# Batched float32 matmul: weight in 24 KB rows through three buffers, its casts cut into quarter-lane pieces on two engines

## The chip, the cores and the metric

One core of a Trainium2 chip runs the kernel. The metric is the device time of one execution in microseconds (us), the median over several runs. Engine names in the profile: PE is TensorE's matmuls, PEld its loads of the stationary operand, DVE is VectorE, ACT is ScalarE, POOL is GpSimd, SP is the queue that issues the transfers.

## The reference

```python
b1, b2, m, k, n = 8, 16, 256, 512, 384
x:      float32 [8, 16, 256, 512]
weight: float32 [8, 16, 512, 384]
np.matmul(x, weight).astype(np.float32)      # 128 independent 256x512 by 512x384 products
```

The inputs are 167.8 MB and the output 50.3 MB.

## The kernel before

It works on groups of G = 4 matrices, 32 groups in all. Each group goes through these steps: SP loads weight (two transfers of 1.5 MB, 12 KB per partition) and x (2 MB, 16 KB per partition); ScalarE casts x to bf16; TensorE transposes it (bf16 pairs as float32 words); VectorE casts the weight and copies ("evacuates") the transposes to `x_t`; TensorE multiplies, four matrices side by side with 32 columns each; ScalarE copies the result out of the accumulators; SP stores it (1.5 MB, 12 KB per partition). The parts that the change touches:

```python
    XS, WS, OS = 2, 2 * G // D, 4        # buffers of x, half groups of weight (D = 2), out
    BS, TS, WBS = 1, 2, 2 * G
    LAG = 4

    def load(e, t, U, s):
        n = t * U + s
        for d in range(G // D):                       # weight, two transfers
            slot = (s * (G // D) + d) % WS
            e.wait_ge(w_cast, ...)                    # the buffer's last casts are done
            e.dma_start(w_sb[slot][:], w_rows[...].rearrange("(p k) n -> p k n", k=S * KO))...
        e.wait_ge(x_cast, n * T + (1 - XS) * T)
        e.dma_start(x_sb[s % XS][:], ...)             # x

    def prepare(e, t, U, s):                          # VectorE
        e.wait_ge(p_made, ...)
        for d in range(G // D):                       # all weight of group n: 8 casts of 64 lanes
            e.wait_ge(w_in[slot], ...)
            for a in range(D):
                for h in range(S):
                    e.tensor_copy(out=w_bf[...][h * HP : (h + 1) * HP], in_=w_sb[slot][...])
        for q in range(T):                            # then the transposes of group n
            e.wait_ge(t_made, n * T + (q + 1 + BIAS))
            e.tensor_copy(out=x_t[...], in_=pt[...])

    # ScalarE, per group: 4 casts of x n, then 4 copies of the products of n
    # TensorE, per group: 16 transposes, then 128 * 4 / 4 = 128 matmuls
    # SP, in a loop: load(n + LAG), then store(n)
```

## Time and profile before

| | before |
|---|---|
| time, median of 3 runs | 518.64 us (518.31 to 518.82) |
| span of the profiled execution | 517.2 us |
| share of the 16 DMA engines in use | 99.3% |
| VectorE, ScalarE, TensorE busy | 64%, 46%, 59% |

The row of the transfer queue says how much of the span packets were in flight, averaged over 16 DMA engines. A group row reads: line, engine, operation, out<-in, shapes, count | busy us, mean ns of one | idle time just before, and what ended it. The lines themselves are in the prediction below.

A transfer runs on 16 DMA engines, and its semaphore is complete only when the last of the 16 has landed. The trace records each of the 16 landings, but not which engine made it. No view of the profile prints these records; the figures for landings below are computed from the packed traces. I call the distance from the middle landing to the last one the **lag**, and the time from one last landing to the next, in queue order, the **late step** of a transfer. In the kernel before, the last x lands at 493.8 us on the middle engine and at 496.6 on the last one: a lag of 2.8 us.

### The profile page before, as it was taken

What the parts mean: (1) busy time and instruction counts of PE and PEld (TensorE: products, weight loads), DVE (VectorE), ACT (ScalarE), POOL (GpSimd) and SP (SyncE); (2) the same over time, 40 slices, a digit from 0 to 9 for tenths busy, and PEclk for the clock granted to TensorE, in tenths of its full rate; (3) what the DMA queues carried; (4) which work ended last, traced back from release to release, by engine and by line L of the source; (5) the groups of instructions that cost most, each with busy time, mean ns of one, the idle gap of its engine ahead of it and who ended that gap; (6) DMA issues with size and microseconds to landing.
All of it is one profiled execution on the core that took longest, in us unless ns stands there. A gap on an engine that the chain in (4) does not pass through costs nothing.

```text
span 517.2 us, 11523 instructions
## 1 busy us (share of the span) xinstructions
PE 306.6 (59%) x4608; PEld 200.6 (39%) x4608; DVE 332.8 (64%) x384; ACT 236.7 (46%) x264; POOL 0.7 (0%) x6
## 2 busy tenths in 40 slices
PE   0478776556665457645577554776446765467752
PEld 0345444334443334433344332444324443244431
DVE  3698875667556676556675566855658656676550
ACT  0465564443644436435355354454444544544441
POOL 0000000000000000000000000000000000000000
PEclk9998877878777887878777778877788877778777
DMA  8999999999999999999999999999999999999996
GB/s 340 430 423 424 424 432 426 429 428 430 432 427 427 427 428 432 429 427 430 426 431 431 426 429 430 427 432 427 427 429 429 427 433 425 430 428 430 429 428 251
DMA packets 18869, 218.18 MB, mean 422 GB/s; under 512 B 2096, under 2 KB 2096, under 8 KB 2608
## 3 DMA queue, kind: packets, MB, share of 16 engines
q1 hardware_dynamic: 18864, 218.11, 99.3%
q8 instruction: 3, 0.05, 0.0%
q14 instruction: 2, 0.02, 0.0%
HBM read 167.77 MB, written 50.33 MB: 422 GB/s over the span
## 4 chain that ended last, share of the span: by engine, by line
DMA 81%; ACT 10%; PE 4%; issue 3%; ACTq 0%; SPq 0%
DMA x_sb<-in_x_dram 81%; ACT x_bf L132 9%; PE po L180 2%; PE pt L166 1%; ACTq L130 0%; ACT out_sb L194 0%; SPq L111 0%; SPq L103 0%; ACT L132 0%; ACTq L193 0%; SPq L282 0%; SPq L55 0%
## 5 line engine op out<-in xcount | busy, mean ns | idle before, releaser
L147 DVE CAST w_bf<-w_sb 64x1536 bf16<-64x1536 f32 x256 | 244.4, 955 | 47.2 <-DMA w_sb<-in_weight_dram 38.5
L166 PE MATMUL pt<-identity,x_bf 128*128 128x128 f32 x512 | 123.7, 425 | 199.3 <-ACT x_bf L132 199.1
L180 PE MATMUL po<-w_bf,x_t 128*32 128x384 bf16 x4096 | 185.1, 342 | 1.0 <-issue 1.0
L166 PEld LDWEIGHTS pt<-identity,x_bf 128*128 128x128 f32 x512 | 91.8, 216 | 232.1 <-issue 218.3
L194 ACT COPY out_sb<-po 128x768 f32<-128x768 f32 x128 | 102.2, 798 | 147.2 <-PE po L180 147.2
L153 DVE COPY x_t<-pt 128x1024 bf16<-128x1024 bf16 x128 | 88.4, 691 | 122.3 <-PE pt L166 121.8
L132 ACT CAST x_bf<-x_sb 128x1024 bf16<-128x1024 f32 x128 | 124.4, 1042 | 80.9 <-DMA x_sb<-in_x_dram 80.8
L180 PEld LDWEIGHTS po<-w_bf,x_t 128*32 128x32 bf16 x4096 | 108.8, 101 | 73.8 <-issue 14.2
L132 ACT ACT_TABLE_LOAD x8 | 10.3, 1283 | 42.9 <-DMA x_sb<-in_x_dram 42.9
masks.py:199 POOL TENSOR_SCALAR_AFFINE_SELECT identity<-identity 128x128 f32<-128x128 f32 x1 | 0.3, 292 | 0.2 <-POOL identity L200 0.2
L200 POOL MEMSET identity<- 128x128 f32 x1 | 0.2, 204 | 0.5 <-SPq L55 0.5
L271 POOL MEMSET const-bfloat16-1.0<- 128x1 bf16 x1 | 0.1, 101 | 0.0
L271 POOL MEMSET const-uint8-127<- 128x1 uint8 x1 | 0.1, 101 | 0.0
L271 POOL MEMSET const-float32-0.0<- 128x1 f32 x1 | 0.1, 98 | 0.2 <-issue 0.2
L271 POOL MEMSET const-float32-1.0<- 128x1 f32 x1 | 0.1, 98 | 0.0
## 6 DMA issues: line engine op xcount, KB each, us to landing
w_sb<-in_weight_dram SPq DMA_DIRECT2D x64, 1536.0 KB, 27.5
x_sb<-in_x_dram SPq DMA_DIRECT2D x32, 2048.0 KB, 27.5
out_dram<-out_sb SPq DMA_DIRECT2D x31, 1536.0 KB, 30.7
out_dram<-out_sb SPq DMA_DIRECT2D x4, 384.0 KB, 5.9
```

The source lines that it names most:

```text
L132: e.copy(out=x_bf[s % BS][:, rows], in_=x_sb[s % XS][:, rows].rearrange("p r (q s c) -> p r s q c", s=S, c=KO),).then_inc(x_cast, 1)
L147: e.tensor_copy(out=w_bf[(s * G + d * D + a) % WBS][h * HP : (h + 1) * HP], in_=w_sb[slot][a * HP : (a + 1) * HP, h * KO : (h + 1) * KO, : ...
L153: e.tensor_copy(out=x_t[s % TS][:, 2 * q : 2 * q + 2], in_=pt[(s * T + q) % PT][:].bitcast(bf16),).then_inc(t_copied, 1)
L166: ins = e.transpose(pt[(s * T + q) % PT][:, rr, h, :], words[:, 2 * q + rr, h :: KO // 2], identity[:],)
L180: ins = e.matmul(po[(s * T + q) % PO][mine, rr, :N], x_t[s % TS][:, 2 * q + rr, ko // 2, mine, ko % 2], w_bf[(s * G + i) % WBS][:, ko, :], ...
L194: e.copy(out=out_sb[s % OS][:, 2 * q : 2 * q + 2, :], in_=po[(s * T + q) % PO][:, :, :N],).then_inc(o_copied, 1)
L200: e.memset(identity[:], 0.0).then_inc(id_done, 1)
L271: nc = _bacc.Bacc("TRN2", target_bir_lowering=False, num_devices=1)
```

## The change

Intent: larger weight rows and weight further ahead of x, paid for with more and smaller casts shared by two engines. The group's weight comes in one transfer of 3 MB with 24 KB per partition into one of three buffers. With this layout a matrix lies on 32 partitions, so a cast covers a quarter of the lanes: 16 per group, 12 on VectorE and 4 on ScalarE. VectorE does one matrix of group n+1, then evacuates group n, then does the other three; ScalarE casts its quarter of weight n+1, then copies out group n, then casts x n+1. `x_t` has one buffer, out three.

```diff
-    XS, WS, OS = 2, 2 * G // D, 4
-    BS, TS, WBS = 1, 2, 2 * G
+    XS, WS, OS = 2, 3, 3
-    LAG = 4
+    LAG = 3
+    U = 6
...
+    def load_w(e, t, U, s):
+        n = t * U + s
+        if not isinstance(n, int) or n >= WS:
+            e.wait_ge(v_cast, (n - WS + 1) * (G * V))
+            e.wait_ge(a_cast, (n - WS + 1) * G)
+        e.dma_start(
+            w_sb[s % WS][:],
+            w_rows[bass.ds(n * (G * K), G * K)].rearrange("(p k) n -> p k n", k=G * KO),
+        ).then_inc(w_in[s % WS], 16)
...
+    def cast_w(e, cast, t, U, s, i, parts, done):
+        for h in parts:
+            cast(
+                out=w_bf[(s * G + i) % (2 * G)][h * C : (h + 1) * C],
+                in_=w_sb[s % WS][i * C : (i + 1) * C, h * KO : (h + 1) * KO, :],
+            ).then_inc(done, 1)
...
     # VectorE
+            for s in range(1, U + 1):
+                cast_w_start(e, t, U, s)             # waits for weight s to land
+                casts(t, U, s, range(1))
+                evacuate(e, t, U, s - 1)
+                casts(t, U, s, range(1, G))
...
     # ScalarE
+        def step(t, U, s, first=False):
+            cast_w_start(e, t, U, s)
+            for i in range(G):
+                cast_w(e, e.copy, t, U, s, i, range(V, G), a_cast)
+            if not first:
+                for q in range(T):
+                    copy_out(e, t, U, s - 1, q)
+            for q in range(T):
+                cast_x(e, t, U, s, q)
```

The order of SP stays: load weight, load x, store. The last group's weight comes in two halves.

More of the change, by code (lines that the diff above doesn't have):

```diff
@@ L43 @@
     T = R // 2
+    NG = B // G
+    V = G - 1
     D = 2
-    S = 2
-    HP = P // D
-    NG = B // G
-    XS, WS, OS = 2, 2 * G // D, 4
-    BS, TS, WBS = 1, 2, 2 * G
+    XS, WS, OS = 2, 3, 3
     PT, PO = 4, 2
-    LAG = 4
+    LAG = 3
+    U = 6
     ctx.enter_context(tc.tile_critical(no_gpsimd_drain=True))
@@ L72 @@
     x_sb = sbuf("x_sb", [P, R, K], fp32, XS)
-    x_bf = sbuf("x_bf", [P, R, S, HP, KO], bf16, BS)
-    x_t = sbuf("x_t", [P, R, KO // 2, P, 2], bf16, TS)
-    w_sb = sbuf("w_sb", [P, S * KO, N], fp32, WS)
-    w_bf = sbuf("w_bf", [P, KO, N], bf16, WBS)
+    x_bf = sbuf("x_bf", [P, R, K], bf16, 1)[0]
+    x_t = sbuf("x_t", [P, R, KO // 2, P, 2], bf16, 1)[0]
+    w_sb = sbuf("w_sb", [P, G * KO, N], fp32, WS)
+    w_bf = sbuf("w_bf", [P, KO, N], bf16, 2 * G)
     out_sb = sbuf("out_sb", [P, R, N], fp32, OS)
@@ L80 @@
     po = psum("po", [P, 2, 512], fp32, PO)
-    id_done, x_cast, w_cast, t_made, t_copied, p_made, o_copied = (
+    id_done, x_cast, v_cast, a_cast, t_made, t_copied, p_made, o_copied = (
         sems(name, 1)[0]
         for name in (
-            "id_done", "x_cast", "w_cast", "t_made", "t_copied", "p_made", "o_copied"
+            "id_done", "x_cast", "v_cast", "a_cast",
+            "t_made", "t_copied", "p_made", "o_copied",
         )
@@ L91, with load_x @@
     x_in, w_in, o_out = sems("x_in", XS), sems("w_in", WS), sems("o_out", OS)
+    w_last = sems("w_last", D)
     BIAS = 8
-    def load(e, t, U, s):
+    def load_x(e, t, U, s):
         n = t * U + s
-        for d in range(G // D):
-            slot = (s * (G // D) + d) % WS
-            if not isinstance(n, int) or n >= 2:
-                e.wait_ge(w_cast, n * (G * S) + ((d + 1) * D * S - 2 * G * S))
-            e.dma_start(
-                w_sb[slot][:],
-                w_rows[bass.ds(n * (G * K) + d * (D * K), D * K)].rearrange(
-                    "(p k) n -> p k n", k=S * KO
-                ),
-            ).then_inc(w_in[slot], 16)
         if not isinstance(n, int) or n >= XS:
-            e.wait_ge(x_cast, n * T + (1 - XS) * T)
+            e.wait_ge(x_cast, (n - XS + 1) * T)
         e.dma_start(
@@ L114, in load, with load_last @@
         ).then_inc(x_in[s % XS], 16)
+    def load_w(e, t, U, s):
[7 more added lines that the diff above has]
+        ).then_inc(w_in[s % WS], 16)
+    def load(e, t, U, s):
+        load_w(e, t, U, s)
+        load_x(e, t, U, s)
+    def load_last(e):
+        n = NG - 1
+        e.wait_ge(v_cast, (n - WS + 1) * (G * V))
+        e.wait_ge(a_cast, (n - WS + 1) * G)
+        for d in range(D):
+            e.dma_start(
+                w_sb[n % WS][:, d * D * KO : (d + 1) * D * KO],
+                w_rows[bass.ds(n * (G * K) + d * D * K, D * K)].rearrange(
+                    "(p k) n -> p k n", k=D * KO
+                ),
+            ).then_inc(w_last[d], 16)
+        load_x(e, 0, NG, n)
     def store(e, t, U, s, pieces=1):
@@ L124, in store, with cast_x @@
             )
-    def cast_x(e, t, U, s, q):
+    def cast_x(e, t, U, s, q, S=G):
         n = t * U + s
@@ L132, in cast_x, with cast_w_start, cast_w_last, evacuate @@
         e.copy(
-            out=x_bf[s % BS][:, rows],
-            in_=x_sb[s % XS][:, rows].rearrange("p r (q s c) -> p r s q c", s=S, c=KO),
+            out=x_bf[:, rows].rearrange("p r (s q c) -> p r s q c", s=S, c=KO),
+            in_=x_sb[s % XS][:, rows].rearrange(
+                "p r (q s c) -> p r s q c", s=S, c=KO
+            ),
         ).then_inc(x_cast, 1)
-    def prepare(e, t, U, s):
+    def cast_w(e, cast, t, U, s, i, parts, done):
[4 more added lines that the diff above has]
+            ).then_inc(done, 1)
+    def cast_w_start(e, t, U, s):
         n = t * U + s
         e.wait_ge(p_made, n * T + (BIAS - T))
-        for d in range(G // D):
-            slot = (s * (G // D) + d) % WS
-            e.wait_ge(
-                w_in[slot], (t * (U * G // D // WS) + s * G // D // WS) * 16 + 16
-            )
-            for a in range(D):
-                for h in range(S):
-                    e.tensor_copy(
-                        out=w_bf[(s * G + d * D + a) % WBS][h * HP : (h + 1) * HP],
-                        in_=w_sb[slot][a * HP : (a + 1) * HP, h * KO : (h + 1) * KO, :],
-                    ).then_inc(w_cast, 1)
+        e.wait_ge(w_in[s % WS], (t * (U // WS) + s // WS) * 16 + 16)
+    def cast_w_last(e, cast, parts, done, by):
+        n = NG - 1
+        e.wait_ge(p_made, n * T + (BIAS - T))
+        H = P // D
+        for d, a in parts:
+            e.wait_ge(w_last[d], 16)
+            for h in range(D):
+                ins = cast(
+                    out=w_bf[(n * G + d * D + a) % (2 * G)][h * H : (h + 1) * H],
+                    in_=w_sb[n % WS][
+                        a * H : (a + 1) * H, (d * D + h) * KO : (d * D + h + 1) * KO, :
+                    ],
+                )
+        ins.then_inc(done, by)
+    def evacuate(e, t, U, s):
+        n = t * U + s
         for q in range(T):
@@ L153, in prepare, with transpose @@
             e.tensor_copy(
-                out=x_t[s % TS][:, 2 * q : 2 * q + 2],
+                out=x_t[:, 2 * q : 2 * q + 2],
                 in_=pt[(s * T + q) % PT][:].bitcast(bf16),
             ).then_inc(t_copied, 1)
-    def multiply(e, t, U, s):
+    def transpose(e, t, U, s, q):
         n = t * U + s
-        words = x_bf[s % BS][:].rearrange("p r s q c -> p r (s q c)").bitcast(fp32)
-        for q in range(T):
-            e.wait_ge(x_cast, n * T + (q + 1))
-            e.wait_ge(t_copied, n * T + (q + 1 - PT + BIAS))
-            for rr in range(2):
-                for h in range(KO // 2):
-                    ins = e.transpose(
-                        pt[(s * T + q) % PT][:, rr, h, :],
-                        words[:, 2 * q + rr, h :: KO // 2],
-                        identity[:],
-                    )
-            ins.then_inc(t_made, 1)
-        e.wait_ge(w_cast, n * (G * S) + G * S)
-        for q in range(T):
-            e.wait_ge(t_copied, n * T + (q + 1 + BIAS))
-            e.wait_ge(o_copied, n * T + (q + 1 - PO + BIAS))
-            for rr in range(2):
-                for ko in range(KO):
-                    for i in range(G):
-                        mine = slice(i * C, (i + 1) * C)
-                        ins = e.matmul(
-                            po[(s * T + q) % PO][mine, rr, :N],
-                            x_t[s % TS][:, 2 * q + rr, ko // 2, mine, ko % 2],
-                            w_bf[(s * G + i) % WBS][:, ko, :],
-                            start=(ko == 0),
-                            stop=(ko == KO - 1),
-                        )
-            ins.then_inc(p_made, 1)
@@ new lines, in transpose, with multiply @@
+        words = x_bf[:].bitcast(fp32)
+        e.wait_ge(x_cast, n * T + (q + 1))
+        e.wait_ge(t_copied, n * T + (q + 1 - PT + BIAS))
+        for rr in range(2):
+            for h in range(KO // 2):
+                ins = e.transpose(
+                    pt[(s * T + q) % PT][:, rr, h, :],
+                    words[:, 2 * q + rr, h :: KO // 2],
+                    identity[:],
+                )
+        ins.then_inc(t_made, 1)
+    def multiply(e, t, U, s, q):
+        n = t * U + s
+        if q == 0:
+            e.wait_ge(v_cast, n * (G * V) + G * V)
+            e.wait_ge(a_cast, n * G + G)
+        e.wait_ge(t_copied, n * T + (q + 1 + BIAS))
+        e.wait_ge(o_copied, n * T + (q + 1 - PO + BIAS))
+        for rr in range(2):
+            for ko in range(KO):
+                for i in range(G):
+                    mine = slice(i * C, (i + 1) * C)
+                    ins = e.matmul(
+                        po[(s * T + q) % PO][mine, rr, :N],
+                        x_t[:, 2 * q + rr, ko // 2, mine, ko % 2],
+                        w_bf[(s * G + i) % (2 * G)][:, ko, :],
+                        start=(ko == 0),
+                        stop=(ko == KO - 1),
+                    )
+        ins.then_inc(p_made, 1)
@@ L205, in on_sync @@
     def on_sync(e):
-        U = OS
         for n in range(LAG):
             load(e, 0, NG, n)
-        rounds = (NG - LAG) // U
+        rounds = (NG - 1 - LAG) // U
         with e.Fori(0, rounds) as t:
@@ L214, in on_sync, with casts @@
         for n in range(rounds * U, NG):
-            if n + LAG < NG:
+            if n + LAG < NG - 1:
                 load(e, 0, NG, n + LAG)
+            elif n + LAG == NG - 1:
+                load_last(e)
             store(e, 0, NG, n, T if n == NG - 1 else 1)
         for s in range(OS):
-            e.wait_ge(o_out[s], 16 + 16 * (NG // OS + (T - 1 if s == (NG - 1) % OS else 0)))
+            used = len(range(s, NG, OS)) + (T - 1 if s == (NG - 1) % OS else 0)
+            e.wait_ge(o_out[s], 16 + 16 * used)
     def on_vector(e):
-        U = 2
         e.sem_inc(t_copied, BIAS)
-        with e.Fori(0, NG // U) as t:
-            for s in range(U):
-                prepare(e, t, U, s)
+        def casts(t, U, s, matrices):
+            for i in matrices:
+                cast_w(e, e.tensor_copy, t, U, s, i, range(V), v_cast)
+        cast_w_start(e, 0, NG, 0)
+        casts(0, NG, 0, range(G))
+        with e.Fori(0, (NG - 2) // U) as t:
+            for s in range(1, U + 1):
[3 more added lines that the diff above has]
+                casts(t, U, s, range(1, G))
+        evacuate(e, 0, NG, NG - 2)
+        cast_w_last(e, e.tensor_copy, ((0, 0), (1, 0), (1, 1)), v_cast, G * V)
+        evacuate(e, 0, NG, NG - 1)
     def on_tensor(e):
@@ L236, in on_tensor @@
             for s in range(U):
-                multiply(e, t, U, s)
+                for q in range(T):
+                    transpose(e, t, U, s, q)
+                for q in range(T):
+                    multiply(e, t, U, s, q)
     def on_scalar(e):
-        U = OS
         e.sem_inc(o_copied, BIAS)
@@ L243, in on_scalar @@
             e.sem_inc(o_out[s], 16)
-        with e.Fori(0, NG // U) as t:
-            for s in range(U):
-                for q in range(T):
-                    cast_x(e, t, U, s, q)
-                for q in range(T):
-                    copy_out(e, t, U, s, q)
+        def step(t, U, s, first=False):
+            cast_w_start(e, t, U, s)
+            for i in range(G):
+                cast_w(e, e.copy, t, U, s, i, range(V, G), a_cast)
+            if not first:
+                for q in range(T):
+                    copy_out(e, t, U, s - 1, q)
+            for q in range(T):
+                cast_x(e, t, U, s, q)
+        step(0, NG, 0, first=True)
+        with e.Fori(0, (NG - 2) // U) as t:
+            for s in range(1, U + 1):
+                step(t, U, s)
+        cast_w_last(e, e.copy, ((0, 1),), a_cast, G)
+        for q in range(T):
+            copy_out(e, 0, NG, NG - 2, q)
+        for q in range(T):
+            cast_x(e, 0, NG, NG - 1, q, D)
+        for q in range(T):
+            copy_out(e, 0, NG, NG - 1, q)
     on_gpsimd(nc.gpsimd)
```

## The prediction

> **What bounds the kernel now.** I read the page from the top, then the chain, then stretches of the span, and last the packets. The page's share rows show that no engine is near its limit: TensorE is busy for 59% of the span, VectorE for 64%, ScalarE for 46%. The queue row is different:
>
> ```profile
> q1 hardware_dynamic: 18864, 218.11, 99.3%
> HBM read 167.77 MB, written 50.33 MB: 422 GB/s over the span
> DMA 81%; ACT 10%; PE 4%; issue 3%; ACTq 0%; SPq 0%
> ```
>
> The reader is to see 99.3%: packets were in flight for practically the whole span on all 16 DMA engines. The chain that ended last agrees, 81% of it is loads of x. Is there room at the ends? The view by stretches has the start, the middle, the time from the last landing of x, and the drain; the columns are the stretch, its length, the busy time of PE, PEld, DVE, ACT and POOL, the clock, the DMA share and GB/s:
>
> ```profile
> 0.00:20.00 20.00, 0.15 (x1) 0.16 (x2) 7.64 (x8) 2.62 (x3) 0.70 (x6) 1.00 0.89 369
> 60.00:260.00 200.00, 120.84 (x1853) 79.00 (x1846) 132.67 (x153) 94.60 (x106) 0.00 (x0) 0.79 1.01 429
> 260.00:460.00 200.00, 124.93 (x1844) 81.60 (x1848) 131.35 (x152) 92.98 (x104) 0.00 (x0) 0.78 1.01 429
> 496.50:507.70 11.20, 9.04 (x144) 6.26 (x144) 2.77 (x4) 7.06 (x8) 0.00 (x0) 0.79 1.00 425
> 507.70:513.50 5.80, 0.00 (x0) 0.00 (x0) 0.00 (x0) 0.02 (x1) 0.00 (x0) 0.82 0.75 305
> 513.50:517.20 3.70, 0.00 (x0) 0.00 (x0) 0.00 (x0) 0.00 (x0) 0.00 (x0) 0.50 0.03 13
> ```
>
> The middle runs at 429 GB/s with the DMA engines full, and even the last group's work (496.5 to 507.7) has full DMA beside it, as stores are still queued. Only some 2 us at the start, part of 5.8 us in the drain and a fixed 3.7 us at the end are not transfer. The bytes fix the rest: 218.1 MB at 429 GB/s is 508 us. One group of four matrices moves 3.146 MB of weight, 2.097 of x and 1.573 of out, so 7.33 + 4.89 + 3.67 = **15.9 us per group**. That is the period which every engine has to stay under, and 32 of them make the span.
>
> The waits of the transfer queue say the same from its other side: each load waits for a buffer, and then still takes 27.5 us to land where 1.5 MB need 3.7 us. It stands behind some 24 us of queued transfers; that is the slack which a late engine may use up before a DMA engine runs dry.
>
> ```profile
> SPq L103 <- DVE w_bf L147: 269.5, 60, 8.6
> w_sb<-in_weight_dram SPq DMA_DIRECT2D x64, 1536.0 KB, 27.5
> L147 DVE CAST w_bf<-w_sb 64x1536 bf16<-64x1536 f32 x256 | 244.4, 955 | 47.2 <-DMA w_sb<-in_weight_dram 38.5
> L153 DVE COPY x_t<-pt 128x1024 bf16<-128x1024 bf16 x128 | 88.4, 691 | 122.3 <-PE pt L166 121.8
> L132 ACT CAST x_bf<-x_sb 128x1024 bf16<-128x1024 f32 x128 | 124.4, 1042 | 80.9 <-DMA x_sb<-in_x_dram 80.8
> L194 ACT COPY out_sb<-po 128x768 f32<-128x768 f32 x128 | 102.2, 798 | 147.2 <-PE po L180 147.2
> ```
>
> **What the Trainium skill says.** (1) "DMA: Bandwidth & Descriptors", § Where 436 GB/s comes from, puts the fabric ceiling of 16 ports at 435 GB/s; the trace's 429 is 98.6% of it. (2) The same page, § Why small descriptors are slow (HBM only), gives about 3 cycles of overhead per packet, a loss for descriptors of a few hundred bytes. The trace agrees that there is nothing left at 12 KB: the packet records show a median of 460 ns for 12,288 B and 613 ns for 16,384 B, 0.0374 ns per byte in both. (3) "VectorE: DVE Perf Modes", § Two Vector instructions with no wait between them, says that an instruction whose start quadrant differs from the last one's is held until the earlier has finished. Quarter-lane casts change the output quadrant every time; but the half-lane casts of before do too, and eight of them take 7.86 us, 982 ns each against 955 ns alone. So I count 982 ns for a quarter-lane cast as well. (4) "ScalarE: Activation LUTs", § What ACT_TABLE_LOAD costs, gives 186 ns + 0.833 ns per element for a simple activation, and about 93 ns overlap back to back. For 1,024 elements that is 1,039 ns; the trace has 1,042.
>
> **The change, part by part.**
> *Transfers.* Weight comes as 32 loads of 3 MB in 24 KB rows (the last in two halves of 12 KB rows) in place of 64 of 1.5 MB in 12 KB rows. Bytes stay. By (2) a 24 KB packet should take 2 x 460 = 920 ns: gain about zero. Some 31 fewer transfers mean 31 x 16 = 496 fewer semaphore packets at 9 ns (packet records), over 16 engines 0.3 us. The order in the queue is still weight n, x n, store; one store fewer (LAG 3, was 4) now comes ahead of the last x.
> *VectorE.* A cast's length goes by its elements per lane, 1,536 in both, so halving the lanes doubles the count: 16 quarter casts per group, of which VectorE takes 12. Before, 8 x 0.982 + 4 x 0.69 = 10.6 us per group. After, 12 x 0.982 + 4 x 0.72 (0.69 and a small gap) = 11.8 + 2.9 = **14.7 us**, under 15.9.
> *ScalarE.* It gains 4 quarter casts. Estimate from the fit in (4): 186 + 0.833 x 1,536 = 1,466 ns, four of them 4 x 1.466 - 3 x 0.093 = 5.6 us. With 3.9 us for the four x casts (as the timeline shows them) and 4 x 0.8 = 3.2 for the copies, 12.7 us busy per group, before 7.1. Its order is now weight casts n+1, copies n, x casts n+1, so there is a loop through TensorE: weight casts 5.6; copies of two output tiles, the third and fourth tile only then made (1.35 us each), their copies: about 4.9; x casts 3.9. Together some **14.4 us** per group, plus 1.28 us of table load once in 6 groups. Under 15.9 again.
> *Where these lie.* Let x n land at time L. Weight n+1 lands one store and one weight load later, at L + 11. VectorE casts the first matrix until L + 14, evacuates the transposes until L + 17, casts the rest until L + 25.8; the next weight lands at L + 26.9. ScalarE casts until L + 16.7, copies until L + 21.5, casts x n+1 until L + 25.4, also in time. So both still wait for weight, with about 1.1 to 1.5 us to spare, and x is released 9.5 us after it landed in place of 4. The queue held some 24 us of work; that delay is absorbed. At the start five loads (13.6 MB, 32 us) are queued at once, and the third x is released at about 22 us by my count, before they run out.
> *The end.* One store fewer ahead of the last x: it lands 3.7 us later (about 500.2), with three stores queued behind it (11.0 us), in place of four. The last group's work took 11.2 us before (496.5 to 507.7) and its order is unchanged: last copy at about 511.4, its store's 0.9 us and a receipt of a few us after it. The transfers alone give 500.2 + 11.0 + 3.7 = 514.9, by the same sum as before (496.5 + 14.7 + 3.7). So the end moves by between 0 and +1 us.
>
> **Sum:** 518.6 - 0.3 (semaphore packets) + 0.3 (end, about a third of its width) + 0 (middle, bound by transfers) = **518.6 us**.
>
> **Rivals.**
> 1. *Larger rows lift the transfer rate.* The weight is 100.7 of 218.1 MB. For: it is what one would hope of 24 KB rows. Against: equal ns per byte at 12 and 16 KB, and only 6 GB/s left up to the ceiling in (1). Even at 435 GB/s for all bytes the gain is 508 - 501 = 7 us, 1.4%, still within 2%.
> 2. *VectorE or ScalarE becomes the bound.* For: 14.7 and 14.4 of 15.9 us leave some 8%, and the two engines now wait for each other through TensorE. A quarter cast of 1.1 us in place of 0.98 would make VectorE's group 16.1 us and the time some 525; ordering losses of 1.5 us a group, 32 x 0.5 = 16 us over the 1.0 to spare, give 530 to 535. If quarter casts lost their rate [...], VectorE would need over 20 us a group and the kernel some 700 us. Against: shape and layout in a lane are those of before, only lanes differ.
> 3. *Fewer buffers starve the queue* (out_sb 3 for 4, x_t 1 for 2). For: a store takes 30.6 us to land and out_sb is reused sooner. Against: by the schedule above a store is issued 25.4 us after its L and lands at about L + 51; the copy that reuses its buffer comes at L + 47.7 + 16.7, 13 us later. It would show as copies waiting for a store, and cost some us a group if it happened.
>
> **Range and chances.** The middle can hardly get faster: -2.6 us allows for slightly faster rows and a better drain. Above, +4 us allows a rougher start, a longer end or an occasional late engine. So 516.0 to 522.5 should hold it 8 times in 10. Faster by 2% needs under 508, below the bytes at today's rate with no start or end: 0.02. Slower by 2% (over 529) needs rival 2 or 3: 0.08. Within 2%: 0.90.
>
> **What would show it.** Right: DMA share of 1.01 and 428 to 431 GB/s in the middle; 24 KB packets at about 920 ns; VectorE at about (12 x 955 + 4 x 691) x 32 ns = 455 us busy, 88% of the span; ScalarE at 390 to 420 us; quarter casts still waiting for weight. Wrong: a DMA share clearly under 1.0 in the middle, VectorE over 95% busy, quarter casts on VectorE over 1.05 us or on ScalarE over 1.6 us, copies to out_sb waiting for stores, or transfer queue waits with landings well under 20 us.

## The result, and the profile after

The changed kernel takes **523.80 us** (median of 4 runs, 523.34 to 523.86), the kernel before 518.67 us in the same rounds. The ratio of the changed kernel to the kernel before is 1.0100 (95% interval 1.0085 to 1.0115). Ratios here are the mean time of one kernel's runs over that of the other's of the same rounds, so they are not quite the ratio of the medians. "Within 2%" was right; the time lies 1.3 us above the predicted range of 516.0 to 522.5, and 5.2 us above the predicted 518.6.

The page of the changed kernel, queue row, chain and groups:

```profile
q1 hardware_dynamic: 14400, 218.11, 98.0%
DMA 57%; PE 15%; DVE 9%; ACT 9%; issue 8%; SPq 1%; ACTq 0%; DVEq 0%
...
L163 DVE CAST w_bf<-w_sb 32x1536 bf16<-32x1536 f32 x372 | 353.8, 951 | 67.7 <-DMA w_sb<-in_weight_dram 56.9
...
L163 ACT CAST w_bf<-w_sb 32x1536 bf16<-32x1536 f32 x124 | 182.1, 1468 | 13.4 <-DMA w_sb<-in_weight_dram 10.5
```

A quarter-lane cast takes what was predicted: 951 ns on VectorE, 1,468 on ScalarE (estimate 1,466). VectorE is busy for 84% of the span, ScalarE for 79%. But the DMA share fell from 99.3 to 98.0%. The view by stretches (columns as in the prediction) says where:

```profile
60.00:260.00 200.00, 136.91 (x1808) 82.92 (x1808) 176.29 (x203) 164.93 (x154) 0.00 (x0) 0.76 1.01 430
260.00:460.00 200.00, 138.13 (x1836) 82.28 (x1840) 173.29 (x202) 160.30 (x150) 0.00 (x0) 0.74 1.01 431
...
500.00:512.00 12.00, 9.95 (x146) 6.32 (x144) 8.46 (x10) 9.01 (x10) 0.00 (x0) 0.79 0.55 230
512.00:522.10 10.10, 5.44 (x130) 3.36 (x128) 0.73 (x2) 3.19 (x4) 0.00 (x0) 1.00 0.41 162
```

The middle is as full as before, even a little faster (430 to 431 GB/s, was 429). The loss shows in the last 22 us, where the DMA engines are half idle; in the kernel before they were full until 507.7 us of 517.2. The timeline of the end (start, length, engine, group, and in brackets the idle time before it and what ended it), first the changed kernel and then the kernel before:

```profile
482.68 2.91 DVE L163 CAST w_bf<-w_sb 32x1536 bf16<-32x1536 f32 x3 [1.77 <-DMA w_sb<-in_weight_dram]
...
486.37 7.83 PE L222 MATMUL po<-w_bf,x_t 128*32 128x384 bf16 x128 [2.96 <-DVE x_t L192]
...
495.08 3.89 ACT L154 CAST x_bf<-x_sb 128x1024 bf16<-128x1024 f32 x4
...
507.12 3.89 ACT L154 CAST x_bf<-x_sb 128x1024 bf16<-128x1024 f32 x4
...
517.50 0.80 ACT L236 COPY out_sb<-po 128x768 f32<-128x768 f32 x1 [0.50 <-PE po L222]
```

```profile
496.66 3.89 ACT L132 CAST x_bf<-x_sb 128x1024 bf16<-128x1024 f32 x4 [3.83 <-DMA x_sb<-in_x_dram]
...
506.92 0.80 ACT L194 COPY out_sb<-po 128x768 f32<-128x768 f32 x1 [0.50 <-PE po L180]
```

The last copy ends at 518.3 us, not at the predicted 511.4. The chain to it starts with the weight of group 30, which VectorE receives at 482.7 us; from there matmuls 29, casts of x 30, matmuls 30, casts of x 31 and matmuls 31 follow each other. The landing records show why that weight is so late:

| landing, us | middle engine | second to last | last engine |
|---|---|---|---|
| weight 30, after | 474.6 | 476.7 | **482.7** |
| last x, after | 495.4 | 497.4 | **503.7** |
| last x, before | 493.8 | 495.7 | 496.6 |

Fifteen of the DMA engines are at most about 2 us behind the middle one, in both kernels. One is 8.3 us late in the changed kernel. Everything waits for it. That it is the same engine all the time is read from the lag, which grows steadily while the other fifteen keep together. The lag grows by about 0.27 us per group from group 8 on, and all of it in stores: in groups 10 to 26 the late step of a store is 3.96 us, the second to last engine's 3.70. Loads of weight and x take the late engine as long as the others.

The 4.9 us between the two spans add up from these records: the last x is preceded by one store more (+3.7 us), comes 2.1 us sooner on the middle engine (24 KB packets take 912 ns, twice 12 KB would be 920), and its lag is 8.3 in place of 2.8 us (+5.5). So it lands 7.2 us later (496.55 to 503.71). From there to the end it is 18.4 us in place of 20.6 (-2.2). Without the added lag the sum would be some 5.5 us smaller, an estimate that takes the other terms as they are.

### The profile page after: what moved, and what is told of

Read it like the earlier page. It is cut to its first block, busy times and chain, and to the rows that moved or that the text cites. A ratio compares the mean times of both kernels' runs of the same rounds, so it can differ in the third digit from the quotient of the medians.

```text
span 522.1 us, 11674 instructions
## 1 busy us (share of the span) xinstructions
PE 343.3 (66%) x4608; PEld 208.6 (40%) x4608; DVE 439.5 (84%) x506; ACT 412.6 (79%) x383; POOL 0.7 (0%) x6
## 4 chain that ended last, share of the span: by engine, by line
DMA 57%; PE 15%; DVE 9%; ACT 9%; issue 8%; SPq 1%; ACTq 0%; DVEq 0%
DMA w_sb<-in_weight_dram 57%; PE po L222 13%; DVE w_bf L163 6%; ACT x_bf L154 6%; DVE x_t L192 2%; ACT w_bf L163 2%; PE pt L204 1%; ACT out_sb L236 1%; SPq L106 1%; SPq L144 0%; ACTq L152 0%; SPq L116 0%; DVEq L191 0%; ACTq L314 0%; ACTq L170 0%
## 5 line engine op out<-in xcount | busy, mean ns | idle before, releaser
L163 DVE CAST w_bf<-w_sb 32x1536 bf16<-32x1536 f32 x372 | 353.8, 951 | 67.7 <-DMA w_sb<-in_weight_dram 56.9
L222 PE MATMUL po<-w_bf,x_t 128*32 128x384 bf16 x4096 | 227.6, 394 | 80.2 <-DVE x_t L192 76.5
L222 PEld LDWEIGHTS po<-w_bf,x_t 128*32 128x32 bf16 x4096 | 125.0, 115 | 182.2 <-DVE x_t L192 88.3
L163 ACT CAST w_bf<-w_sb 32x1536 bf16<-32x1536 f32 x124 | 182.1, 1468 | 13.4 <-DMA w_sb<-in_weight_dram 10.5
L204 PE MATMUL pt<-identity,x_bf 128*128 128x128 f32 x512 | 115.8, 382 | 93.9 <-ACT x_bf L154 93.6
L204 PEld LDWEIGHTS pt<-identity,x_bf 128*128 128x128 f32 x512 | 83.6, 213 | 126.2 <-issue 125.4
L154 ACT CAST x_bf<-x_sb 128x1024 bf16<-128x1024 f32 x128 | 124.4, 1042 | 0.8
L192 DVE COPY x_t<-pt 128x1024 bf16<-128x1024 bf16 x128 | 80.1, 684 | 5.5 <-PE pt L204 4.3
L180 DVE CAST w_bf<-w_sb 64x1536 bf16<-64x1536 f32 x6 | 5.7, 955 | 0.1
L180 ACT CAST w_bf<-w_sb 64x1536 bf16<-64x1536 f32 x2 | 2.9, 1469 | 0.0
```

The lines of the kernel that those rows point to most:

```text
L154: e.copy(out=x_bf[:, rows].rearrange("p r (s q c) -> p r s q c", s=S, c=KO), in_=x_sb[s % XS][:, rows].rearrange("p r (q s c) -> p r s q c ...
L163: cast(out=w_bf[(s * G + i) % (2 * G)][h * C : (h + 1) * C], in_=w_sb[s % WS][i * C : (i + 1) * C, h * KO : (h + 1) * KO, :],).then_inc(do ...
L180: ins = cast(out=w_bf[(n * G + d * D + a) % (2 * G)][h * H : (h + 1) * H], in_=w_sb[n % WS][a * H : (a + 1) * H, (d * D + h) * KO : (d * D ...
L192: e.tensor_copy(out=x_t[:, 2 * q : 2 * q + 2], in_=pt[(s * T + q) % PT][:].bitcast(bf16),).then_inc(t_copied, 1)
L204: ins = e.transpose(pt[(s * T + q) % PT][:, rr, h, :], words[:, 2 * q + rr, h :: KO // 2], identity[:],)
L222: ins = e.matmul(po[(s * T + q) % PO][mine, rr, :N], x_t[:, 2 * q + rr, ko // 2, mine, ko % 2], w_bf[(s * G + i) % (2 * G)][:, ko, :], sta ...
```

## The experiments

Seventeen profiles exist in all: before, after, and fifteen experiments. The variants of the changed kernel start from a form in which three waits of the SP queue are written as `n * T + constant`; `control` is that form alone. The runs went to four chips; the late engine showed on each.

This table holds what the runs gave. "In it" counts the matmuls that start within the late engine's store; late step and count are means over groups 10 to 26; lag is that of the last x. Runs marked "one run" have no interval. Three runs with many short instructions follow in the text, as their instructions do not last over groups 10 to 26.

| run | time, us | ratio to before | late step of a store, us | matmuls in it | lag, us |
|---|---|---|---|---|---|
| before | 518.7 | | 3.73 | 10 | 2.8 |
| after | 523.8 | 1.0100 | 3.96 | 62 | 8.3 |
| control | 523.8 | 1.0102 | 3.96 | 62 | 9.0 |
| rows12 | 526.3 | 1.0144 | 3.96 | 61 | 9.0 |
| no_act_w (one run, wrong result) | 523.2 | | 3.94 | 59 | 7.9 |
| dma24 (one run, wrong result) | 523.4 | | 3.70 | 0 | 1.8 |
| dma_pe (one run, wrong result) | 534.9 | | 4.09 | 91 | 13.5 |
| dma_act (one run, wrong result) | 638.9 | | 3.70 | 0 | 2.2 |
| dma_dve (one run, wrong result) | 523.8 | | 3.70 | 0 | 2.2 |
| evac_first (one run) | 520.0 | | 3.78 | 30 | 5.0 |
| store_mid | 521.3 | 1.0046 | 3.76 | 6 | 3.9 |
| store_mid_evac | 526.5 | 1.0144 | 4.01 | 63 | 10.4 |
| before_mid | 530.3 | 1.0231 | 4.15 | 86 | 14.3 |
| store_mid_tail | 518.8 | 1.0013 | 3.76 | 6 | 4.1 |

### First round: rows, ScalarE, or the DMA engines alone

**control**: waits rewritten, same values.

```diff
-            e.wait_ge(x_cast, (n - XS + 1) * T)
+            e.wait_ge(x_cast, n * T + (1 - XS) * T)      # and the two waits of load_w alike
```

> The changed kernel, with three waits of the transfer queue written as n*T + constant in place of (n - 1)*T: the same values, so the same schedule. It is the base of all variants. All theories: 523.3 to 524.2 us; last landing of the last x some 8 us behind the middle one of its 16 DMA engines (503.7 against 495.4 us).

It gave 523.78 us and a lag of 9.0 us: a fair base.

**rows12**: the same buffers, but two transfers of 12 KB rows per group.

```diff
-        e.dma_start(w_sb[s % WS][:], w_rows[...].rearrange("(p k) n -> p k n", k=G * KO))...
+        rows = w_rows[...].rearrange("(p k) n -> p k n", k=G * KO)
+        for d in range(D):
+            half = slice(d * D * KO, (d + 1) * D * KO)
+            e.dma_start(w_sb[s % WS][:, half], rows[:, half]).then_inc(w_in[s % WS], 16)
```

> The changed kernel with each group's weight loaded in two transfers of 12 KB rows into the same buffer, all else kept. Theory A (one of the 16 DMA engines falls behind, and the 24 KB rows are why): the lag of the last landing of the last x falls from 8.3 to about 3 us, and the time to 518.5 to 519.5 us. Theory A2 (one DMA engine falls behind for another reason): lag stays 7 to 9 us, time 523.5 to 525.5 us, as 12 KB rows cost 0.05 us more per group. Theory B (the end of the kernel is long because the last groups' work now comes after weight casts, whatever the landings do): 523.5 to 525.5 us whatever the lag is.

The lag stays at 9.0 us, so theory A falls: the row size is not the cause. The time rises by 2.5 us over control, 0.8 us more than the top of what A2 allowed; the middle engine's last x came 1.9 us later (497.3 for 495.4). That is what the 24 KB rows are worth.

**no_act_w**: ScalarE casts no weight.

```diff
-            for i in range(G):
-                cast_w(e, e.copy, t, U, s, i, range(V, G), a_cast)
+            e.sem_inc(a_cast, G)
```

> Wrong result on purpose: ScalarE casts no weight (the quarter of each weight that it made stays zero), but still waits for the weight to land. Takes 5.9 us per group off ScalarE. Theory A2 (lag comes from the DMA engines themselves): lag stays about 8 us, the last x still lands at about 503.5 us, and the time is 518.5 to 520.5 us as only what follows that landing is left (15 us). If ScalarE's reads of the weight buffers slow one DMA engine: lag under 4 us, time 516 to 518.5 us. Theory B alone: lag does not matter, 517 to 519 us.

The lag is still 7.9 us, so ScalarE's reads are not the cause. The time hardly moved (523.17, one run), which no theory had: with 5.9 us per group off ScalarE the last x still landed at 503.6 us, as A2 said, but its casts began only at 506.5, because VectorE still took its first cast of weight 30 at 482.6 us and evacuated group 29 behind it. The chain of the end hangs on the last landing of weight 30, not on ScalarE.

**dma24**: the changed kernel's transfers alone, paced by landings, no other engine at work. The result is zeros.

```diff
-            e.wait_ge(x_cast, ...)                     # load_x
+            e.wait_ge(x_in[s % XS], ...)               # load_w and store alike; on_vector, on_tensor
                                                        # and on_scalar are not called
```

> Wrong result on purpose (zeros): only the transfers of the changed kernel in the same order, from the same buffers, each paced by landings, with no other engine at work. Theory A or A2 with the cause in the DMA engines: the last engine's lag grows to 6 to 9 us by the last x and its stores take some 0.2 us longer than the others'. If the other engines' work causes the lag: it stays at 1.5 to 3.5 us. Time 512 to 518 us either way.

The stretches of this run (columns: stretch, length, POOL busy, clock, DMA share, GB/s):

```profile
0.00:10.00 10.00, 8.05 (x7) 1.00 0.00 0
...
260.00:460.00 200.00, 0.00 (x0) 1.00 1.01 431
460.00:521.60 61.60, 0.00 (x0) 1.00 0.95 405
```

The first 10 us clear the output tiles, so the transfers need some 511 us of the 521.6. With them the time missed the expected 512 to 518 us. The rate is the changed kernel's, and the lag is 1.8 us (one run): it does not come from the DMA engines by themselves. Something that goes with the other engines' work makes it.

### Second round: which engine does it

In the kernel before, late stores 28 and 29 took 4.04 and 4.00 us while the last matmuls ran, and store 30, after them, 3.71. In the changed kernel the matmuls of a group run right when the late engine stores. So the suspect was the coincidence of store and matmul. Three runs add one engine's work to dma24, back to back and with nothing waiting for it.

```diff
+    def on_tensor(e):                                  # dma_pe
+        with nc.Fori(0, 44, ...) as t:
+            ... 256 matmuls like the kernel's, on constant tiles
```

> Wrong result on purpose: the transfers alone, as in the run before, with TensorE doing the kernel's matmuls back to back on constant tiles all the while (nothing waits for it). So far: in the changed kernel one of the 16 DMA engines takes 3.95 us for a store where the others take 3.68, in the stores that coincide with matmuls and output copies; in the transfers alone none does. Theory C1 (matmuls, which read the on-chip memory, slow stores, which read it too): store steps of 3.85 to 4.0 us for the last engine or for all, its lag over 4 us by the end. C2 (ScalarE's output copies do it) or C3 (VectorE's casts do it): 3.65 to 3.72 us, lag under 2.5 us.

```diff
+    def on_scalar(e):                                  # dma_act
+        with e.Fori(0, 150) as t:
+            for q in range(T): e.copy(out=scratch[:, 2 * q : 2 * q + 2, :], in_=po[q % PO][:, :, :N])
```

> Wrong result on purpose: the transfers alone, with ScalarE copying from the accumulators to a tile of its own, back to back. C2: store steps of 3.85 to 4.0 us and a lag over 4 us. C1 or C3: 3.65 to 3.72 us and a lag under 2.5 us.

```diff
+    def on_vector(e):                                  # dma_dve
+        with e.Fori(0, 40) as t:
+            ... 12 casts like the kernel's quarter casts, from a tile of its own
```

> Wrong result on purpose: the transfers alone, with VectorE doing the changed kernel's quarter casts back to back from a tile of its own. C3: store steps of 3.85 to 4.0 us and a lag over 4 us. C1 or C2: 3.65 to 3.72 us and a lag under 2.5 us.

The stretches of dma_pe (columns: PE, PEld, DVE, POOL busy, clock, DMA share, GB/s):

```profile
260.00:460.00 200.00, 200.00 (x4930) 130.63 (x4924) 0.00 (x0) 0.00 (x0) 1.00 1.01 430
460.00:520.00 60.00, 8.33 (x208) 5.19 (x196) 0.00 (x0) 0.00 (x0) 0.60 0.91 389
520.00:533.00 13.00, 0.00 (x0) 0.00 (x0) 0.00 (x0) 0.00 (x0) 0.50 0.32 136
```

TensorE alone is enough. In stores 10 to 24, the ones that lie beside matmuls, the late step is 4.15 us with 100 to 104 matmuls in each; in the two after the matmuls had ended it is 3.67, so that the table's mean is 4.09. The lag is 13.5 us, and the run ends 11.5 us later than dma24 with one engine's backlog (32% of the DMA engines in use, then idle). Stores on the second to last engine run beside the same matmuls and take 3.70 us. ScalarE's copies and VectorE's casts leave the late step at 3.70 and the lag at 2.2 us. (The dma_act run is 638.9 us long only because I gave it too many copies; its transfers end at 521 us.) C1 stands in so far as it is TensorE; C2 and C3 fall.

**evac_first** changes the order on VectorE, so that the matmuls of group n do not wait for weight n+1.

```diff
-                cast_w_start(e, t, U, s)
-                casts(t, U, s, range(1))
-                evacuate(e, t, U, s - 1)
-                casts(t, U, s, range(1, G))
+                e.wait_ge(p_made, (t * U + s) * T + (BIAS - T))
+                evacuate(e, t, U, s - 1)
+                cast_w_start(e, t, U, s)
+                casts(t, U, s, range(G))
```

> The changed kernel with one change of order on VectorE: the transposes of group n are evacuated before the first cast of group n+1, not after it, so that the matmuls of group n need not wait for the weight of group n+1 to land. Theory D (this wait ties the matmuls to the last landing, so that the late engine's stores fall on them in every group): matmuls start some 3 us earlier, fewer of the late engine's stores coincide with them, lag 3 to 7 us, and the time 519 to 522.5 us. If the order is of no consequence: 523 to 524.5 us and lag 8 us. If VectorE loses more than it can spare (its slack is some 1.5 us per group): over 525 us.

As expected: 30 matmuls in the late store in place of 62, a late step of 3.78 us, lag 5.0, time 520.0 us (one run; before took 518.15 in one run on that chip). The first engine to land now had 55 matmuls in its stores and still took 3.64 us: being beside matmuls does not slow every engine.

### Third round: move the store, and what about the matmul it is

**store_mid** moves one issue: the store goes between weight and x.

```diff
-                load(e, t, U, LAG + s)
-                store(e, t, U, s)
+                load_w(e, t, U, LAG + s)
+                store(e, t, U, s)
+                load_x(e, t, U, LAG + s)
...                                                    # the tail after the loop alike
```

> The changed kernel with one issue moved: the store of group n goes into the transfer queue between the weight and the x of group n + 3, not after both. Theory C1 (matmuls slow the stores of one DMA engine where they coincide): the matmuls of a group start 3.7 us after the last landing of the next weight, so a store that directly follows that weight is over before them; the late engine's store step falls from 3.94 to 3.7 us, its lag at the last x from 8.3 to under 3.5 us, and the time to 517.3 to 519 us. If the lag has another cause, or is of no consequence for the time: 522.5 to 525 us.

The matmuls in a late store fall from 62 to 6, the late step to 3.76 us, and the lag to 3.9 us; 3.7 and under 3.5 were expected, and what the rest comes from was not tested. The time falls by 2.5 us to 521.26, less than the 517.3 to 519 expected. I had not counted that the last x now stands behind one store more: its casts waited for it until 503.6 us.

**store_mid_evac** puts both edits together.

> As store_mid, and VectorE evacuates the transposes of group n before the first cast of group n + 1, as in evac_first. Theory C1: matmuls start earlier, partly beside the store again: lag 2 to 5 us, time 516 to 519.5 us. It is the candidate to beat both kernels if the end gets shorter by more than the lag costs.

This miss is telling. Both edits help alone, and together they are worse than the changed kernel: 526.54 us, lag 10.4. The late engine's store now fills the 4 us right after the last landing of the weight (it ended 8.8 us after it in the changed kernel), and the matmuls start some 1 us after that landing in place of 3.7. So they meet again, with 63 matmuls in a late store and a late step of 4.01 us. The step goes with the count of matmuls in the store, whichever edit made it.

**dma_pe_short** has the same number of matmuls as dma_pe, with 32 moving columns in place of 384, so they run through in 115 us (7 to 122 us).

```diff
-                                po[q % PO][mine, rr, :N], ..., w_bf[0][:, ko, :],
+                                po[q % PO][mine, rr, :32], ..., w_bf[0][:, ko, :32],
```

> Wrong result on purpose: as dma_pe, with the same number of matmuls, but 32 moving columns each in place of 384, so TensorE executes as many or more instructions per us and reads a small part of the data per us. If the late engine is slowed by the reading of moving data: store step of the last engine 3.68 to 3.75 us and lag under 3 us. If by TensorE's instructions themselves, or their fetching or stationary loads: a step of 4.0 us or more while they run and a lag over 6 us.

In the two stores that lay wholly beside them the late step was 7.03 and 7.11 us, with 721 and 740 matmuls, and 3.69 us after them; the lag ended at 14.7. The time was 535.8 us (one run). The same number of instructions cost about the same lag as in dma_pe, with a twelfth of the moving data. It is not the moving data. The excess over 3.70 us, divided by the matmuls in the store, is 4.2 ns each in the changed kernel, 4.4 in dma_pe and 4.6 here, for counts from 62 to 740 (2.7 to 5.2 over all runs with 30 or more in a store).

### Fourth round: the other kernel, and instructions or memory

**before_mid** makes the store_mid edit in the kernel before.

> The kernel before, with its store moved between the weight and the x of the same loop step. Theory C1 (one DMA engine's stores are slowed by matmuls that run during them): before, the late engine's stores held 10 matmuls each (its step 3.73 us); moved to just ahead of the next x they fall on the previous group's matmuls, 5 to 10.5 us after the last x landed: over 40 matmuls in a store, a step of 3.85 to 3.95 us, and a lag at the last x of 5 to 9 us in place of 2.8. Time 519.5 to 523 us. If C1 is wrong: lag 2 to 3.5 us, time 518 to 519.5 us.

The kernel before becomes 12 us slower by moving one issue: 530.29 us, ratio 1.0231 (1.0214 to 1.0248). Lag and time went the way of C1 and far past my sizes. The matmuls follow the last landing, so the later the late engine is, the more surely they fall on its store: 86 on average. In the stretches of this run (columns as in the prediction) the end is drained by one engine:

```profile
500.00:512.00 12.00, 6.50 (x130) 3.54 (x128) 8.49 (x10) 3.57 (x5) 0.00 (x0) 0.78 0.68 285
512.00:528.50 16.50, 10.41 (x144) 6.52 (x144) 2.77 (x4) 6.76 (x8) 0.00 (x0) 0.71 0.28 111
```

**dma_pe_rows32** has the instructions of dma_pe_short on 32 partitions in place of 128.

```diff
-                                x_t[:, ...], w_bf[0][:, ko, :32],
+                                x_t[:32, ...], w_bf[0][:32, ko, :32],
```

> Wrong result on purpose: as dma_pe_short (its late engine fell back by some 12 us while 11264 short matmuls ran), with operands on 32 partitions in place of 128: the same number of TensorE instructions, a quarter of the on-chip memory read, none of it in three of four partition groups. Theory E (it is the instructions, for instance their fetching over the same DMA engine, and not what they read): lag 11 to 16 us as before. Theory F (what the stationary and moving loads read from on-chip memory slows a DMA engine that reads there): lag under 7 us.

The lag is 14.8 us again (late step 7.09 and 7.00 us in the two stores wholly beside them, 536.2 us in one run). Three quarters of the on-chip memory reads are gone and nothing changed, so theory F falls.

**dma_dve_short** lets VectorE run 5,120 copies of 8 elements.

```diff
+        with e.Fori(0, 40) as t:
+            e.wait_ge(a_cast, t * 128 + 128)
+            for i in range(128):
+                e.tensor_copy(out=scratch[1][:, i], in_=scratch[0][:, i]).then_inc(a_cast, 1)
```

> Wrong result on purpose: the transfers alone, beside 5120 tiny VectorE copies of 8 elements, some 70 to 100 ns each, on tiles of their own. Theory E in its wide form (any engine's instruction stream costs one DMA engine time during its stores, by its rate): one DMA engine falls back, by an estimate from dma_pe (0.41 us per store at some 50 instructions per us) of about 0.1 us per store at 12 per us: last store step 3.75 to 3.85 us while they run, lag 3.5 to 6 us. If only TensorE does this: step 3.70 us and lag under 2.5 us.

The row of these copies, 5,120 of them, busy for 381.5 us:

```profile
L167 DVE COPY scratch<-scratch 128x8 f32<-128x8 f32 x5120 | 381.5, 194 | 1.7 <-DVEq L163 0.3
```

The lag is 5.1 us, and the late step averages 3.85 us between 200 and 410 us. In dma_dve 480 large casts over more time left it at 3.70. So the number of instructions, of VectorE too, is what these runs point to: theory E in its wide form, for VectorE on one run of each kind.

**store_mid_tail** puts the last x of store_mid ahead of store 28 again.

```diff
                 load_last(e)
+                load_x(e, 0, NG, n + LAG)
             store(e, 0, NG, n, T if n == NG - 1 else 1)
-            if n + LAG < NG:
+            if n + LAG < NG - 1:
                 load_x(e, 0, NG, n + LAG)
```

> As store_mid, but the last x goes ahead of the store of group 28 again. In store_mid the last x landed 3.7 us later, as one more store was ahead of it, and its casts waited 1.1 us for it. Expected: last x lands at 499.5 to 500.5 us, its casts start when ScalarE is through with the copies of group 30, and the time is 519.5 to 520.8 us (store_mid 521.3). No gain if the end hangs on ScalarE and TensorE alone.

The last x lands at 499.8 us and the time is 518.82 us, 0.7 us better than expected. Against the kernel before in the same rounds the ratio is 1.0013 with an interval of 0.9996 to 1.0029. So moving one issue and keeping the last x in front takes back all of the change's loss. It does not beat the kernel before. Its DMA share is still 0.63 in the last 17 us:

```profile
500.00:517.00 17.00, 9.61 (x180) 6.19 (x168) 5.00 (x7) 8.69 (x10) 0.00 (x0) 0.99 0.63 258
```

### What is shown, and what stays open

Shown: one of the 16 DMA engines takes longer for a store while TensorE executes many instructions; it is a matter of how many, not of how much they read; and removing the coincidence removes most of the lag and, with the last x kept in front, the loss. For VectorE the same was seen in one run. Loads are not slowed: the weight load after store 1 of dma_pe_short held 764 matmuls and took the late engine 7.28 us, the second to last 7.23.

Why a number of instructions should slow a store is open. My first guess was the fetching of instructions. The Trainium skill, "Runtime: NRT & Kernel Launch", § Instruction fetch mechanics, says that each sequencer drives a DMA queue of its own to fetch the next page while it executes, in blocks of 16 KiB or 256 instructions, and calls the cost mostly hidden. By that page 11,264 matmuls with their 11,264 stationary loads would be 88 blocks if every block were fetched anew, an estimate. The trace speaks against it. Its rows for packets of kind "instruction" in dma_pe_short are these:

```profile
q8 instruction: 3, 0.05, 0.0%
q14 instruction: 1, 0.01, 0.0%
```

The three packets of 16 KB start at 8.1, 14.7 and 23.6 us and the other at 123.7, while the lag grew between 63 and 125 us. In the changed kernel the last of six such packets is at 101.7 us, and the lag still grows in store 27, which lands at 491 us. So fetching is not the cause, unless the trace misses most of its packets.

A rival that no run here tests is the profiler itself. The trace holds a record of each instruction, so records grow with instructions as the lag does. Every run lists a span and a granted clock, which come from such records; as far as the record tells, no time here was taken without the profiler. Whether the late engine exists without it stays open, and a run without it would tell.

One more point is not shown. The first stores hold many matmuls too (stores 0 to 7 of the changed kernel 45 to 72, stores 0 to 3 of dma_pe 88 to 92) and have a late step of only 3.60 to 3.79 us. It would fit if the slow engine first has to fall behind the others before it is the last to land, but the records do not name the engines.

## Why the prediction was wrong

- **What bounds the middle: right.** DMA share 1.01 and 430 to 431 GB/s, inside the 428 to 431 given.
- **24 KB packets: right, but small sizes add up.** 912 ns, predicted 920. The prediction counted this as no gain; rows12 shows that it gives 1.9 us at the last x. That it offset part of the loss at the end was luck.
- **VectorE and ScalarE: right.** 951 and 1,468 ns a cast; VectorE 439.5 us busy (455 predicted), ScalarE 412.6 (390 to 420 predicted). One term was low: four quarter casts of ScalarE take 5.95 us in a row (5.6 predicted). The overlap of 93 ns that the sum took off shows in the x casts, four of 1,042 ns in 3.89 us, but not in these. Neither engine became the bound in the middle; rival 2 did not happen.
- **Buffers: right.** No copy waited for a store; rival 3 did not happen.
- **The end: wrong, and this step failed.** It read "it lands 3.7 us later (about 500.2)", "last copy at about 511.4" and "the end moves by between 0 and +1 us". Two terms were mis-sized. First, the last x landed at 503.7 us. The step took all 16 DMA engines to move alike, and one of them lagged by 8.3 us. Second, its casts began 3.4 us after it landed, because the chain of three groups had started late, on the same engine's landing of weight 30. So the third of the "three stores queued behind it" was issued only at 507.1 us, and the DMA engines ran half empty. The step's own "order is unchanged" held for group 31 alone.
- **The schedule had the cause in view.** It placed the matmuls of a group just behind the landing of the next weight, and so beside the next store. I read from that only that the engines were in time. That instructions could go with a slow store was in none of the rivals.
- **The margin of the range.** "+4 us allows a rougher start, a longer end": the longer end alone took 5.2. Without the added 5.5 us of lag the time would be near 518.3 us by the sum above, an estimate; store_mid_tail, with 4.1 us of lag, ran in 518.8.

## What to carry to other kernels

When a kernel is bound by transfers, look at the landing of each of the 16 DMA engines, not only at the mean rate: every wait is for the last one, and 8 us of lag on one engine hide behind a DMA share of 1.01. When instruction-heavy work follows a landing, ask which transfer runs beside it; a store placed there let one engine fall behind in every group, and moving one issue changed the time by 2.5 us in one kernel and 12 us in the other. As far as the record tells, all this was measured with the profiler on, so compare times without it before you reorder a kernel for it. And once transfers are saturated, a change of buffers or rows can gain little in the middle, so count the end of the kernel with the work of the last three groups, not of the last alone.

## What the Trainium skill lacked or had wrong

- No page says that the number of instructions on an engine can go with one late DMA engine. Here 22,528 short TensorE instructions, or 5,120 of VectorE, went with a lag of 14.7 and 5.1 us, against 1.8 us without them. The cause is not shown.
- "DMA: Bandwidth & Descriptors", § Latency and other measured facts, knows of two DMA engines that are usually slower and ties this, as a best guess, to the descriptor rings of transfers issued from GpSimd. Here all transfers are issued from SP, and one engine is slower only in stores, and only beside many instructions: 3.70 us without, 3.96 us in the changed kernel, 7.03 and 7.11 us beside short matmuls. The records do not say which engine it is.
- No page has the lag between the engines of one transfer as a quantity to watch: 2.8 us before, 8.3 us after, 14.3 us in before_mid.
